# Attention: q and k kept by halves of the sequence, the first pair's groups as q, k, k, q, scores nine steps ahead of the values

## The chip, the cores and the metric

The kernel runs on one core of one Trainium2 chip. A core has five engines that each work through their own list of instructions in order: TensorE (PE, matmuls and transposes), VectorE (DVE), ScalarE (ACT), GpSimd (POOL) and SyncE (SP, which issues the DMAs here). They meet at semaphores. On-chip memory is SBUF (128 partitions) and PSUM (where PE writes, in banks of 512 fp32 columns).

The metric is the time of one execution on the device, in microseconds (us). The kernel before takes 2181.59 us, the median of 3 executions between 2181.50 and 2181.69.

## The reference

A decoder trunk of two layers on one sequence of 1024 tokens, width 1024, in fp32. Layer 0 mixes the tokens with a gated recurrent block, layer 1 with stick-breaking attention (16 heads of 64); a dense SwiGLU block of 2816 stands behind each. The change touches only the attention:

```python
def stick_breaking_attention(x, w_qkv, w_o):
    qkv = jnp.einsum("bsd,de->bse", x, w_qkv).reshape(bsz, seq, 3, N_HEADS, HEAD_DIM)
    q, k, v = ...
    for blk in range(seq // Q_BLOCK):        # Q_BLOCK = 128
        t0, t1 = blk * Q_BLOCK, (blk + 1) * Q_BLOCK
        z = jnp.einsum("bhqd,bhkd->bhqk", q[:, :, t0:t1], k[:, :, :t1]) * scale
        strict = jnp.arange(t1)[None, :] < t0 + jnp.arange(Q_BLOCK)[:, None]
        log_fail = jnp.where(strict, jax.nn.log_sigmoid(-z), 0.0)
        suffix = lax.cumsum(log_fail, axis=3, reverse=True) - log_fail
        weights = jnp.where(strict, jnp.exp(jax.nn.log_sigmoid(z) + suffix), 0.0)
        outs.append(jnp.einsum("bhqk,bhkd->bhqd", weights, v[:, :, :t1]))
    o = ...
    return jnp.einsum("bse,ed->bsd", o, w_o)
```

## The kernel before

**Precision.** An fp32 product is made of three matmuls: each operand is split into a part `hi` that PE's fp32r format holds and a remainder `lo`, and PE adds hi·hi, hi·lo and lo·hi (`mm3`, lines 141 to 143). Splitting takes a cast on ACT (`hi`) and a subtraction on DVE (`lo`).

**Two streams on PE.** The attention works through 8 pairs of heads. Two kinds of work are woven together by hand: the *fill*, which makes q, k and v of the next pair, and the *iterations*, which make scores, weights and values of the current pair. The whole stretch stands in a `manual_schedule` (line 1619): each engine executes its instructions in the order in which the Python code emits them, with no scheduler between.

**The fill** is the generator `qkv_steps` (line 1410). A pair has six groups: q, k and v (`which` 0, 1, 2), each for two halves of the sequence (`n`, 512 tokens). A group has 8 steps, a step is one `mm3` of 512 columns, so a pair has 48 steps. At the start of each `which`, `next_weights` queues the splitting of the weight block that comes next (three pieces in the list `later`, of which one is emitted per step), and `load_link` issues the load of the block after that, `raw` (three buffers). Behind a group `evacuate` (line 1440) takes the sum out of PSUM: DVE multiplies by `rbc[n]` (the row's 1/rms, spread over the partitions) into `t`; one step later ACT and DVE split `t` into `two`, and four DMAs on SP's queue spread it: q's into the tiles `Q` (lines 1466 and 1467; hi on 64 partitions and lo on the other 64, for each of the two heads), k's into `KK` (line 1470; hi and lo side by side, the same on both halves of the partitions). One score is then two matmuls that contract over all 128 partitions.

**An iteration** of the main loop (line 1645) emits, in this order: the score matmuls of one *chunk* (`z_part`, into one of two PSUM banks of the pool `psZ`); the PE transposes of a *unit* of weights two iterations ahead of its use (`t_part`) and their split (`t_split`: cast `th` on ACT, subtraction `tl` on DVE); the chunk's sigmoid on ACT and scan on DVE (`z_rest`, lines 1516 to 1522); one piece from `later`; two fill steps; in the last pair, steps of the output projection (`out_fill`) as `amount` says; an extra chunk in the iterations listed in `gains`; and the value matmuls of the unit (`av_part`). A head has 12 chunks (`chunk_list`, line 1494): eight on the diagonal, for query blocks j = 0 to 7 (those with j ≥ 4 read the second half of q and of k), then four off the diagonal, with the second half of q and the first of k. A head also has 12 units. `LEAD` says how many iterations the chunks run ahead of the units: 8, and by the three `gains` 11 within the last pair.

**The start.** Before the main loop the first pair's fill runs alone for 34 steps (line 1631), as nothing else is there to do: q half 0 and 1, k half 0 and 1, and two steps of v. The row statistics are not ready when q's groups end, so q's evacuations are put off (`waiting`) and the table `between` emits them at set steps: statistics at 12 and 16, the spreading of the result (`broadcast_r`) at 17 and 21, q's evacuations at 18 and 22. q's groups take the two `psZ` banks, which are idle then; k's and v's use the pool `psQ`.

## Time and profile before

| | |
|---|---|
| device time, median of 3 | 2181.59 us (2181.50 to 2181.69) |
| the profiled execution's own time | 2181.29 us |
| its span in the profile | 2179.5 us |
| granted clock of TensorE, mean | 0.999 |
| bytes moved by DMA | 277.64 MB, mean 127 GB/s |
| waits of `qk_ps` matmuls (the fill) on anything, largest group | 0.0 us |
| transfers `kk<-two` (64, 256 KB each) | 3.9 us from issue to landing |
| transfers `q<-two` (64, 128 KB each) | 2.3 us from issue to landing |

The span is the time from the first to the last instruction that the profiler saw. In the rows that follow, a busy time is the time in which an engine had an instruction in work. A row of the timeline has start and duration in us, engine, operation with its line, and the tiles written and read (`out<-in`); what stands in brackets behind it is the idle time of that engine just ahead, and what ended it. A row by stretches has the window, its length, and then for each engine (PE, its weight loads, DVE, ACT, POOL) the busy time and the count of instructions; behind these the granted clock, the share of the DMA engines that was busy, and GB/s. In a row on DMA issues, the first three times are the issue's own in ns, and the line under it the time to landing. The attention lies between 970 and 1450 us.

### The profile page before, as it was taken

The page shows a single profiled execution, that of the slowest core. Times are in us where ns is not written, and L with a number is a line of the kernel's source. Part 1 is how long each engine was busy: PE and PEld are TensorE (multiplying, and loading weights), DVE is VectorE, ACT ScalarE, POOL GpSimd, SP SyncE. Part 2 cuts the span into 40 slices and gives each one's busy share as a digit, 9 for nine tenths or more (in the row PEclk, how much of TensorE's full clock was granted, in tenths as well). Part 3 has the DMA queues.
Part 4 walks back from the last instruction along what each step waited for, and adds up shares of the span by engine and source line. Part 5 has one row for each costly group of instructions (what it writes and reads, how often), then busy time and mean ns, then how long its engine had stood idle before and what let it go on. Part 6 is the DMA issues. An engine that isn't in the chain of part 4 may idle for free.

```text
span 2179.5 us, 27426 instructions
## 1 busy us (share of the span) xinstructions
PE 2165.6 (99%) x10126; PEld 1802.2 (83%) x10126; DVE 1703.6 (78%) x2380; ACT 1077.0 (49%) x1765; POOL 112.2 (5%) x84
## 2 busy tenths in 40 slices
PE   8999999999999999999999999999999999999998
PEld 7888888888888888888888888888888888888887
DVE  7888777767777887887888888886877777788886
ACT  6677445334444544554555555553534444454556
POOL 1222020000000000000000000002000000000002
PEclk9999999999999999999999999999999999999999
DMA  7111412344444764434333344552133444467452
GB/s 233 49 49 39 135 39 73 103 125 157 138 146 139 248 222 130 146 121 101 98 97 93 95 105 107 147 193 57 53 116 122 146 145 145 141 232 233 138 153 89
DMA packets 296101, 277.64 MB, mean 127 GB/s; under 512 B 15256, under 2 KB 210976, under 8 KB 295968
## 3 DMA queue, kind: packets, MB, share of 16 engines
q1 hardware_dynamic: 295808, 275.64, 41.1%
q8 instruction: 79, 1.29, 0.3%
q14 instruction: 54, 0.44, 0.1%
q10 hardware_dynamic: 160, 0.27, 0.0%
HBM read 175.71 MB, written 74.97 MB: 115 GB/s over the span
## 4 chain that ended last, share of the span: by engine, by line
PE 96%; DVE 2%; ACT 1%; DMA 1%; issue 0%; SPq 0%; DVEq 0%; ACTq 0%
PE p_ps L143 18%; PE p_ps L141 18%; PE p_ps L142 18%; PE qk_ps L141 4%; PE qk_ps L143 4%; PE qk_ps L142 4%; PE wt_ps L1533 3%; PE a_ps L142 3%; PE a_ps L143 3%; PE a_ps L141 3%; PE ob_ps L141 3%; PE ob_ps L142 2%; PE ob_ps L143 2%; PE z_ps L1503 2%; PE z_ps L1504 2%; PE av_ps L1555 2%
## 5 line engine op out<-in xcount | busy, mean ns | idle before, releaser
L143 PE MATMUL p_ps<-vh,wbl 128*128 128x512 f32 x524 | 204.2, 390 | 0.2 <-DVE wbl L721 0.2
L143 PE MATMUL p_ps<-vh,wal 128*128 128x512 f32 x524 | 204.1, 389 | 0.1
L141 PE MATMUL p_ps<-vh,wbh 128*128 128x512 f32 x524 | 204.2, 390 | 0.0
L141 PE MATMUL p_ps<-vh,wch 128*128 128x512 f32 x524 | 204.1, 390 | 0.0
L143 PE MATMUL p_ps<-vh,wcl 128*128 128x512 f32 x524 | 204.1, 389 | 0.0
L142 PE MATMUL p_ps<-vl,wbh 128*128 128x512 f32 x524 | 203.9, 389 | 0.0
L142 PE MATMUL p_ps<-vl,wch 128*128 128x512 f32 x524 | 203.9, 389 | 0.0
L142 PE MATMUL p_ps<-vl,wah 128*128 128x512 f32 x524 | 203.9, 389 | 0.0
L141 PE MATMUL p_ps<-vh,wah 128*128 128x512 f32 x524 | 203.8, 389 | 0.0
L1542 ACT CAST th<-wt_ps 128x512 fp32r<-128x512 f32 x192 | 92.1, 480 | 209.6 <-PE wt_ps L1533 209.5
L717 ACT CAST wbh<-sb 128x1024 fp32r<-128x1024 f32 (+2 forms) x69 | 69.6, 1009 | 194.1 <-DVE sb L701 194.1
L1543 DVE TENSOR_TENSOR tl<-wt_ps,th 128x512 fp32r<-128x512 f32 x192 | 106.1, 552 | 62.9 <-ACT th L1542 61.1
L141 PE MATMUL qk_ps<-vh,whi 128*128 128x512 f32 x264 | 118.3, 448 | 0.0
L143 PEld LDWEIGHTS p_ps<-vh,wbl 128*128 128x128 f32 x524 | 98.4, 188 | 21.9 <-DVE wbl L721 1.5
L143 PEld LDWEIGHTS p_ps<-vh,wal 128*128 128x128 f32 x524 | 98.4, 188 | 21.4 <-DVE wal L712 1.0
L143 PEld LDWEIGHTS p_ps<-vh,wcl 128*128 128x128 f32 x524 | 98.4, 188 | 21.0 <-DVE wcl L731 0.6
L141 PEld LDWEIGHTS p_ps<-vh,wch 128*128 128x128 f32 x524 | 98.4, 188 | 20.5 <-ACT tb L1108 0.2
L141 PEld LDWEIGHTS p_ps<-vh,wbh 128*128 128x128 f32 x524 | 98.4, 188 | 20.4 <-ACT ta L1108 0.2
L142 PEld LDWEIGHTS p_ps<-vl,wah 128*128 128x128 f32 x524 | 98.4, 188 | 20.4
L141 PEld LDWEIGHTS p_ps<-vh,wah 128*128 128x128 f32 x524 | 98.4, 188 | 20.4
L142 PEld LDWEIGHTS p_ps<-vl,wbh 128*128 128x128 f32 x524 | 98.4, 188 | 20.3
L142 PEld LDWEIGHTS p_ps<-vl,wch 128*128 128x128 f32 x524 | 98.4, 188 | 20.3
(353 smaller groups left out, 5568.2 us busy)
## 6 DMA issues: line engine op xcount, KB each, us to landing
raw<-in_ffn_w_in SPq DMA_DIRECT2D x88, 512.0 KB, 4.0
vl<-pd SPq DMA_DIRECT2D x128, 256.0 KB, 3.5
pd<-U SPq DMA_DIRECT2D x90, 256.0 KB, 2.3
kk<-two SPq DMA_DIRECT2D x64, 256.0 KB, 3.9
raw<-in_ffn_w_out SPq DMA_DIRECT2D x56, 256.0 KB, 3.4
raw<-in_attn_w_qkv SPq DMA_DIRECT2D x24, 512.0 KB, 4.3
q<-two SPq DMA_DIRECT2D x64, 128.0 KB, 2.3
raw<-in_lru_w_in SPq DMA_DIRECT2D x15, 512.0 KB, 4.1
```

Of the source, the lines that this page charges most:

```text
L141: nc.tensor.matmul(ps, lhsT=wh, rhs=mh, start=first, stop=False, **kw)
L142: nc.tensor.matmul(ps, lhsT=wh, rhs=ml, start=False, stop=False, **kw)
L143: nc.tensor.matmul(ps, lhsT=wl, rhs=mh, start=False, stop=last, **kw)
L717: nc.scalar.copy(self.full(self.wb), self.full(self.sb))
L1503: nc.tensor.matmul(ps[:, 0 : c1 - c0], lhsT=lhsT, rhs=KK[q][hx][:, 0, c0:c1], start=True, stop=False)
L1504: nc.tensor.matmul(ps[:, 0 : c1 - c0], lhsT=lhsT, rhs=KK[q][hx][:, 1, c0:c1], start=False, stop=True)
L1533: nc.tensor.transpose(tp[:, c : c + P], W[q, hx, j, kb // 4][:, (kb % 4) * P : (kb % 4 + 1) * P], ident)
L1542: nc.scalar.copy(th[:, q0:], tp[:, q0:])
L1543: nc.vector.tensor_sub(tl[:, q0:], tp[:, q0:], f32(th)[:, q0:])
L1555: nc.tensor.matmul(ps[:, q0:], lhsT=VV[q][:, kb, hx], rhs=tl[:, q0:], start=False, stop=last)
```

## The change

The tiles of q and k are cut in two, one per half of the sequence: `Q[q]` of 1024 columns with four buffers becomes `Q[q, n]` of 512 with eight, `KK[q]` of 2 x 1024 likewise `KK[q, n]` of 2 x 512. A k transfer therefore writes one run of 1024 fp32 on each of 64 partitions, and no longer two runs of 512. The bytes, the number of DMAs, matmuls and other instructions stay.

In the first pair the groups run in the order q half 0, k half 0, k half 1, q half 1, v. The two first ones, q half 0 and k half 0, are put off and wait in `psZ`; q half 1 is evacuated in the ordinary way. The loads and splits of coming weight blocks move along with the groups. The first fill loop has 32 steps, `LEAD` is 9, and there are two extra chunks, so that the lead within the last pair is 11 as before.

```diff
         def qkv_steps(q):
-            for which in range(3):
-                w, at = wq.pop((q, which)), 3 * q + which + 1
-                if at < 3 * NP:
-                    wq[divmod(at, 3)] = next_weights(raws.pop(at))
+            groups = [(which, n) for which in range(3) for n in range(NH)]
+            if q == 0:
+                groups[1:4] = groups[2], groups[3], groups[1]
+            w = {}
+            for which, n in groups:
+                if which not in w:
+                    w[which] = wq.pop((q, which))
+                if n == 0 if q or which == 2 else (which, n) in ((0, 0), (0, 1)):
+                    at = 3 * q + which + 1 + (n if q == 0 else 0)
+                    if at < 3 * NP:
+                        wq[divmod(at, 3)] = next_weights(raws.pop(at))
+                    else:
+                        mix[0].w[mix[0].order[0]] = next_weights(mix[0].raw.pop(0))
+                    for i in (at + 1,) if at < 3 * NP else (at + 1, at + 2):
+                        load_link(i)
+                early = q == n == 0 and which < 2
+                ks = (1, 5, 2, 6, 3, 7, 0, 4) if (q, which) == (0, 0) else range(ND)
+                pool, tag = (psZ, "z") if early else (psQ, "qk")
+                ps = pool.tile([P, NB], F32, tag=tag, name="qk_ps")
+                wh, wl = w[which]
+                for i, k in enumerate(ks):
+                    mm3(ps, wh[:, k], wl[:, k], xh[k][n], xl[k][n], i == 0, i == ND - 1)
+                    if i == 5 and late:
+                        late.pop()()
+                    if i < ND - 1:
+                        yield
+                ev = evacuate(q, which, n, ps)
+                if early:
+                    waiting.append(ev)
+                    yield
                 else:
-                    mix[0].w[mix[0].order[0]] = next_weights(mix[0].raw.pop(0))
-                for i in (at + 1,) if at < 3 * NP else (at + 1, at + 2):
-                    load_link(i)
-                ks = (1, 5, 2, 6, 3, 7, 0, 4) if (q, which) == (0, 0) else range(ND)
-                for n in range(NH):
-                    pool, tag = (psZ, "z") if (q, which) == (0, 0) else (psQ, "qk")
-                    ps = pool.tile([P, NB], F32, tag=tag, name="qk_ps")
-                    for i, k in enumerate(ks):
-                        mm3(ps, w[0][:, k], w[1][:, k], xh[k][n], xl[k][n], i == 0, i == ND - 1)
-                        if i == 5 and late:
-                            late.pop()()
-                        if i < ND - 1:
-                            yield
-                    ev = evacuate(q, which, n, ps)
-                    if (q, which) == (0, 0):
-                        waiting.append(ev)
-                        yield
-                    else:
-                        next(ev)
-                        yield
-                        next(ev, None)
+                    next(ev)
+                    yield
+                    next(ev, None)
         def evacuate(q, which, n, ps):
-            full = lambda tag, m: [ap.tile([P, m, S], F32R, tag=tag, name=tag, bufs=4) for _ in range(2)]
+            halves = lambda tag, m: [ap.tile([P, m, NB], F32R, tag=tag, name=tag, bufs=8) for _ in range(2)]
             t = ap.tile([P, NB], F32, tag="t", name="t", bufs=2)
             cs = slice(n * NB, (n + 1) * NB)
             if which == 2:
@@ -1453,21 +1463,21 @@
             else:
                 nc.vector.tensor_mul(t, ps, rbc[n])
                 yield
-            if which == 0 and n == 0:
-                Q[q] = [t[:, 0] for t in full("q", 1)]
-            if which == 1 and n == 0:
-                KK[q] = full("kk", 2)
+            if which == 0:
+                Q[q, n] = [t[:, 0] for t in halves("q", 1)]
+            if which == 1:
+                KK[q, n] = halves("kk", 2)
             if which < 2:
                 two = ap.tile([P, 2, NB], F32R, tag="two", name="two", bufs=2)
                 nc.scalar.copy(two[:, 0], t)
                 nc.vector.tensor_sub(two[:, 1], t, f32(two)[:, 0])
                 for hx, (a, b) in enumerate(((top, bot), (bot, top))):
                     if which == 0:
-                        nc.sync.dma_start(f32(Q[q][hx])[a, cs], f32(two)[a, 0])
-                        nc.sync.dma_start(f32(Q[q][hx])[b, cs], f32(two)[a, 1])
+                        nc.sync.dma_start(f32(Q[q, n][hx])[a], f32(two)[a, 0])
+                        nc.sync.dma_start(f32(Q[q, n][hx])[b], f32(two)[a, 1])
                     else:
                         for half_ in (top, bot):
-                            nc.sync.dma_start(f32(KK[q][hx])[half_, :, cs], f32(two)[a])
+                            nc.sync.dma_start(f32(KK[q, n][hx])[half_], f32(two)[a])
                 return
             if n == 0:
                 VV[q] = ap.tile([P, NT, 2, P], F32R, tag="v", name="v", bufs=2)
@@ -1499,9 +1509,11 @@
         def z_part(q, hx, j, ci, c0, c1, diag):
             nk = (j + 1) * P
             ps = psZ.tile([P, NB], F32, tag="z", name="z_ps")
-            lhsT = Q[q][hx][:, j * P : (j + 1) * P]
-            nc.tensor.matmul(ps[:, 0 : c1 - c0], lhsT=lhsT, rhs=KK[q][hx][:, 0, c0:c1], start=True, stop=False)
-            nc.tensor.matmul(ps[:, 0 : c1 - c0], lhsT=lhsT, rhs=KK[q][hx][:, 1, c0:c1], start=False, stop=True)
+            lhsT = Q[q, j // 4][hx][:, j % 4 * P : (j % 4 + 1) * P]
+            for i in range(2):
+                nc.tensor.matmul(
+                    ps[:, 0 : c1 - c0], lhsT=lhsT, rhs=KK[q, ci][hx][:, i, 0 : c1 - c0], start=i == 0, stop=i == 1
+                )
             return ps
@@ -1587,7 +1599,7 @@
         heads = [(q, hx) for q in range(NP) for hx in range(2)]
         chunks = [c for q, hx in heads for c in chunk_list(q, hx)]
         units = [u for q, hx in heads for u in unit_list(q, hx)]
-        LEAD = 8
+        LEAD = 9
         def all_fill():
             yield from first
@@ -1626,17 +1638,17 @@
                 16: lambda: stats(rbc[1], psO, "o", 1),
                 17: lambda: broadcast_r(psO, "o", 0),
                 18: lambda: [*waiting[0]],
+                19: lambda: [*waiting[1]],
                 21: lambda: broadcast_r(psO, "o", 1),
-                22: lambda: [*waiting[1]],
             }
-            for i in range(1, 2 * ND * NH + 3):
+            for i in range(1, 2 * ND * NH + 1):
                 next(first)
                 if i in between:
                     between[i]()
-                if i > 4 and later:
+                if i > 3 and later:
                     later.pop(0)()
-            gains = [len(units) - x for x in (31, 29, 27)]
+            gains = [len(units) - x for x in (31, 28)]
             last_two, out_work = len(units) - 2 * 12, out_fill()
             amount = {x: 2 for x in (-1, 0, 1, 9, 10, 11, 12)}
```

What it does to the order, at three places. **SP, first pair.** SP issues the DMAs one after the other; `q` and `kk` are transfers of q and k into their tiles, `raw` the loads of weight blocks, `hd` belongs to the residual stream. Before:

```order
L114 DMA raw_7661<-in_attn_w_qkv 128x8x128
L1092 DMA hd0_1_121<-h0_1_1900 128x512
L1092 DMA hd4_0_128<-h4_0_1907 128x512
L1466 DMA q_7679<-two_7681 64x512
L1467 DMA q_7679<-two_7681 64x512
L1466 DMA q_7680<-two_7681 64x512
L1467 DMA q_7680<-two_7681 64x512
L1466 DMA q_7679<-two_7711 64x512
L1467 DMA q_7679<-two_7711 64x512
L1466 DMA q_7680<-two_7711 64x512
L1467 DMA q_7680<-two_7711 64x512
L1470 DMA kk_7726<-two_7728 64x2x512 x2
```

With the change:

```order
L1092 DMA hd0_1_121<-h0_1_1900 128x512
L1092 DMA hd4_0_128<-h4_0_1907 128x512
L1476 DMA q_7674<-two_7676 64x512
L1477 DMA q_7674<-two_7676 64x512
L1476 DMA q_7675<-two_7676 64x512
L1477 DMA q_7675<-two_7676 64x512
L1480 DMA kk_7688<-two_7690 64x1024 x2
L1480 DMA kk_7689<-two_7690 64x1024 x2
L1480 DMA kk_7720<-two_7722 64x1024 x2
L1480 DMA kk_7721<-two_7722 64x1024 x2
L114 DMA raw_7731<-in_attn_w_qkv 128x8x128
L1476 DMA q_7770<-two_7772 64x512
```

All of k's transfers moved ahead of q's second half, and the load of the next pair's q weights (raw_7661 before, raw_7731 now) moved from ahead of q's transfers to behind k's.

**ACT, the first scores.** `w0`, `w1` and so on are the sigmoids of the first pair's chunks, `whi` the casts of the weight block that SP's list shows as `raw`, `two` the casts of an evacuation. Before:

```order
L1462 CAST two_7762<-t_7760 128x512
L1397 CAST whi_7769<-raw_7661 128x512 x2
L1516 ACT_TABLE_LOAD
L1516 ACTIVATE w0_7786<-z_ps_7783 128x128
L1516 ACTIVATE w1_7799<-z_ps_7796 128x256
L1516 ACTIVATE w2_7811<-z_ps_7808 128x384
L1516 ACTIVATE w3_7827<-z_ps_7824 128x512
```

With the change:

```order
L1528 ACTIVATE w0_7767<-z_ps_7764 128x128
L1472 CAST two_7772<-t_7762 128x512
L1528 ACTIVATE w1_7793<-z_ps_7790 128x256
L1397 CAST whi_7779<-raw_7731 128x512
L1528 ACTIVATE w2_7806<-z_ps_7803 128x384
L1397 CAST whi_7779<-raw_7731 128x512
L1528 ACTIVATE w3_7820<-z_ps_7817 128x512
```

The cast of q's second half and the two casts of the next weight block stood ahead of the first sigmoid and stand between the sigmoids now.

**DVE, k's second half in the second pair.** `t` and `two` are the evacuation's multiplication and subtraction; between them stand the subtraction of a unit (`tl`) and a chunk's scan (`w`). Before:

```order
L1454 TENSOR_TENSOR t_8307<-qk_ps_8232,rbc1_82 128x512
L1543 TENSOR_TENSOR tl_8319<-wt_ps_8314,th_8318 128x384
L1522 SCALAR_TENSOR_TENSOR w_8322<-w_8322,w7_8220 128x512
L1463 TENSOR_TENSOR two_8325<-t_8307,two_8325 128x512
L1543 TENSOR_TENSOR tl_8352<-wt_ps_8348,th_8351 128x256
L1519 SCALAR_TENSOR_TENSOR w0_8355<-w0_8355,unit_7566 128x128
```

With the change:

```order
L1464 TENSOR_TENSOR t_8319<-qk_ps_8244,rbc1_82 128x512
L1555 TENSOR_TENSOR tl_8331<-wt_ps_8326,th_8330 128x384
L1531 SCALAR_TENSOR_TENSOR w0_8334<-w0_8334,unit_7566 128x128
L1473 TENSOR_TENSOR two_8339<-t_8319,two_8339 128x512
L1555 TENSOR_TENSOR tl_8366<-wt_ps_8362,th_8365 128x256
L1531 SCALAR_TENSOR_TENSOR w1_8369<-w1_8369,unit_7566 128x256
```

The chunks moved one iteration forward against the fill, so the scan ahead of the subtraction is that of the next head's first chunk, 128 columns, in place of one of 512.

## The prediction

> **What bounds the kernel now.** I read the busy times first, then the same by stretches, then TensorE (PE) instruction by instruction wherever a stretch is short of full, then the chain of waits behind those places.

> ```profile
> span 2179.5 us, 27426 instructions
> PE 2165.6 (99%) x10126; PEld 1802.2 (83%) x10126; DVE 1703.6 (78%) x2380; ACT 1077.0 (49%) x1765; POOL 112.2 (5%) x84
> ...
> 980.00:990.00 10.00, 8.99 (x43) 7.25 (x42) 4.28 (x7) 4.29 (x8) 0.00 (x0) 1.00 0.93 217
> ...
> 1100.00:1200.00 100.00, 100.00 (x543) 85.00 (x543) 85.84 (x126) 51.41 (x112) 4.57 (x6) 1.00 0.36 95
> ...
> 1425.00:1450.00 25.00, 23.77 (x136) 19.67 (x135) 22.68 (x33) 15.05 (x33) 2.57 (x2) 1.00 0.38 131
> ```

> PE sets the time, and the change leaves it the same matmuls in other places. In the middle of the attention (the row from 1100) it is never idle, so nothing can be won there. Two stretches of the attention are short: one at the first scores, one in the last pair. That caps the gain, so each is read row by row.

> ```profile
> 984.24 0.39 PE L142 MATMUL qk_ps<-xg,whi 128*128 128x512 f32 x1
> 984.47 0.39 PE L143 MATMUL qk_ps<-xg,wlo 128*128 128x512 f32 x1
> 985.86 0.36 PE L1503 MATMUL z_ps<-kk,q 128*128 128x256 f32 x1 [1.01 <-DMA kk<-two]
> ...
> 992.72 0.28 PE L1503 MATMUL z_ps<-kk,q 128*128 128x256 f32 x1
> ```

> Matmuls start every 0.23 us, so the first score could have started at 984.70. It started at 985.86: **1.16 us** lost to the DMA that spreads k.

> ```profile
> 1428.04 0.28 PE L1504 MATMUL z_ps<-kk,q 128*128 128x256 f32 x1
> 1428.63 0.33 PE L1533 MATMUL wt_ps<-ident,w 128*128 128x128 f32 x1 [0.30 <-DVE tl L1543]
> ...
> 1429.26 0.28 PE L1504 MATMUL z_ps<-kk,q 128*128 128x256 f32 x1
> 1429.81 0.66 PE L1533 MATMUL wt_ps<-ident,w 128*128 128x128 f32 x4 [0.26 <-DVE tl L1543]
> ...
> 1430.72 0.34 PE L1504 MATMUL z_ps<-kk,q 128*128 128x384 f32 x1
> 1431.71 0.65 PE L1533 MATMUL wt_ps<-ident,w 128*128 128x128 f32 x4 [0.66 <-DVE tl L1543]
> ```

> From score to transpose 0.59, 0.55 and 0.99 us pass, where some 0.12 to 0.17 would do: **1.7 us** behind VectorE (DVE). Both losses together are 2.9 us, 0.13% of the time.

> **The first scores.** The chain behind the first loss:

> ```profile
> 973.09 0.70 DVE t L1454
> 973.86 0.63 ACT two L1462
> 974.51 0.69 DVE two L1463
> 975.21 1.20 DVE wlo L1398 x2
> ...
> 981.16 0.65 SPq L1470
> 981.86 3.87 DMA kk<-two
> 985.86 0.36 PE z_ps L1503
> ```

> One evacuation is multiply, cast, subtract: 973.09 to 975.20. Before, weights and both halves of q stand ahead of k. Now k's first half is next: multiply at 975.1, cast 975.9, subtract 976.5 to 977.2, first kk DMA at about 977.26. The score needs two DMAs, the second landing 0.70+3.87 us after the first issue: 981.8. PE asks after 32 fill steps in place of 34, two steps of 3 x 0.23 us sooner: 983.3. The data is there 1.5 us early. **Gain 1.16 us**; k half 1's own two land well ahead of its chunk.

> **What is late next.** Moving k forward also moves what stands behind it. The weight block of the next pair (raw_7731) went out before q's DMAs; now it follows all eight of kk. The price of that queue:

> ```profile
> L1470 SPq DMA_DIRECT2D kk<-two x1: 1198/1198/1198, 987.7 to 987.7; - x1
> DMA to landing us min/median/max: 4.8/4.8/4.8
> ...
> L114 SPq DMA_DIRECT2D raw<-in_attn_w_qkv x1: 1321/1321/1321, 990.1 to 990.1; - x1
> DMA to landing us min/median/max: 6.3/6.3/6.3
> ...
> 987.00:992.00 5.00, 5.00 (x25) 4.20 (x24) 3.16 (x5) 1.85 (x5) 0.00 (x0) 1.00 0.98 230
> 992.00:995.50 3.50, 3.50 (x18) 2.92 (x18) 2.46 (x4) 0.82 (x3) 0.00 (x0) 1.00 1.01 280
> ```

> The DMA engines (the share before the last number) are full there. Eight kk transfers took from the first issue, 981.16, to the eighth landing, 987.7+4.8 = 992.5: 11.35 us. The two weight blocks behind them were in at 990.1+6.3 = 996.4, so 1.95 us each. Now the second kk group is ready at 980.1 (copy of rbc1, multiply, cast, subtract: 977.2 + 4 x 0.7), before the first group is through, so the queue does not run dry: eighth kk in at 977.26+11.35 = 988.6, weight block at **990.55**.

> Who waits? ScalarE (ACT) casts half of that block between the second and third sigmoid, and runs in order. Cast and sigmoid:

> ```profile
> 984.83 1.13 ACT L1397 CAST whi<-raw 128x512 fp32r<-128x512 f32 x2
> ...
> 989.73 0.49 ACT L1516 ACTIVATE w<-z_ps 128x384 f32<-128x384 f32 x1 [1.35 <-PE z_ps L1504]
> ```

> So 990.55 + 0.5 + 0.49 = 991.5, when the third chunk's psZ bank comes free; there are two banks, and the fifth chunk takes that one. PE wants it 6.8 us after the first chunk (985.86 to 992.72, less the restart): 983.3+6.8 = 990.1. **Loss 1.4 us.** The fifth chunk also needs q's second half, queued behind the same block: two DMAs of half a kk each, landing around 991.7, the same again and in parallel. The bounds: nothing, if the kk transfers, now one run of 4 KB a partition and not two of 2 KB, went as fast as the weight loads (0.5 MB in 1.95 us, so 0.98 us each and not some 1.18 us [(11.35 - 3.1)/7, a first one landing after 3.1 us]): then all is 1.5 us sooner. At the top 2.0 us, if the second group goes out late. I take 1.4, since both patterns write 64 partitions and the row of the old one is the nearest.

> ```profile
> DMA to landing us min/median/max: 3.1/3.1/3.1
> ```

> [...]

> **One more step of lead.** Score chunks move one iteration forward against the fill, so every k and q is needed one iteration sooner after it is made.

> ```profile
> L1470 SPq DMA_DIRECT2D kk<-two x1: 590/590/590, 1101.5 to 1101.5; - x1
> ...
> 1106.77 0.39 PE L1503 MATMUL z_ps<-kk,q 128*128 128x512 f32 x1
> 1109.23 0.33 PE L1503 MATMUL z_ps<-kk,q 128*128 128x256 f32 x1
> ...
> 1099.63 1.28 DVE L1522 TENSOR_TENSOR_SCAN w<-w,w 128x512 f32<-128x512 f32 x1
> 1100.82 0.67 DVE L1463 TENSOR_TENSOR two<-t,two 128x512 fp32r<-128x512 f32 x1
> ...
> 1101.74 0.42 DVE L1519 TENSOR_TENSOR_SCAN w<-w,unit 128x128 f32<-128x128 f32 x1
> ```

> In pair 2 (counted from 0) k's second half goes out at 1101.5, lands 4.57 us later (as above) at 1106.1, and its first chunk runs at 1109.23: 3.1 us to spare. One iteration costs 2.46 of them. The scan ahead of the subtract is now the short one (0.42 for 1.28 us), which gives 0.86 back. Left: 1.5 us, so pairs 1 to 6 wait for nothing. Without the 0.86 it is 0.7, still cover. The last pair, where chunks come faster:

> ```profile
> 1399.78 3.29 SPq L1470 DMA_DIRECT2D kk<-two  x4
> ...
> 1402.99 0.39 PE L1503 MATMUL z_ps<-kk,q 128*128 128x512 f32 x1
> ```

> Landing 1399.78+4.57 = 1404.35, less 0.86 = 1403.5; the chunk that needs it now stands where an iteration starts at 1402.99, plus 0.23 for the wider chunks ahead (512 columns, two matmuls of 0.23; 256 columns half). **Loss 0.3 us**, bounds 0 and 1.1 (no help from the scan).

> The lead's own benefit is nothing: DVE has slack in the middle (85.84 of 100) and PE no idle time there.

> **The last pair's 1.7 us stay.** The order is the old one again, on every engine, from iteration 166 on (about 1415 us), and DVE comes to rest after that:

> ```profile
> 1426.23 0.69 DVE L1543 TENSOR_TENSOR tl<-wt_ps,th 128x512 fp32r<-128x512 f32 x1 [0.70 <-ACT th L1542]
> ```

> Its 0.70 us of idle just ahead of the stalls wipe out whatever was done sooner. Two extra chunks for three change nothing behind it: 0, bounds -1.7 and +0.5.

> **Sum:** -1.16 + 1.4 + 0.3 + 0 = +0.5 us. The profiled execution took 2181.29 us (1.8 around the span), so 2181.8; the median shown, 2181.59, is 0.3 above it, so 2182.1.

> **Rivals.** (B) The queue clears in time, by the lower bound of the second part: -1.16 + 0.3, **2180.7 us**. For it: one kk DMA came in after 3.1 us and not 4.8, so part of the landing is queueing that a faster run would shorten, and the two weight loads did reach the rate that B needs; against it, those loads wrote 128 partitions, kk writes 64. [...] (C) Slower: k's second half misses its chunk in every pair. Place: the first chunk of 512 to 1023; it decides once the landing slips by more than 1.5 us, for instance because DVE runs its subtract an operation later. Another 1.28 us scan and one kk DMA (1.18) would be 2.5, so 1.0 us of wait in six pairs and 1.1 + 1.0 in the last: 2181.59 + 0.24 + 6.0 + 2.1 = **2189.9 us**. Against it: nothing new stands ahead of that subtract in the order. (D) The last pair's stalls go, since DVE enters it lighter: 2180.7 - 1.7 = **2179.0 us**; against it stands the idle row.

> **How the numbers follow.** Forecast 0.50, B 0.30, C 0.10, D 0.10. The forecast's own range is 2181.0 to 2183.4 (queue 0.7 to 2.0, last pair 0 to 1.1). Both signs hold much of the chance, so the range takes in B and D whole and, at the upper end, the forecast with both bounds and a C that strikes in two pairs only (2183.4 + 2 x 1.0 = 2185.4): 2179.0 to 2185.0; what is left out is most of C. About 0.2% (4.4 us) is what a measurement of this kernel can tell from no change: the forecast, B and D lie within it, C does not. Below 2177.2 no case leads, since the two losses are 2.9 us in all; 0.03 stays there for what I don't see. Slower 0.10, same 0.87.

> **What will show it.** Right: the first score follows the fill with no gap; the third sigmoid runs late, after a cast that waited for the raw DMA, and the fifth chunk's matmul waits 1 to 2 us for ACT or for q; the same three waits stand in the last pair, on DVE. The kk transfers take about 1.2 us each in a burst. Wrong: no wait at the fifth chunk (B), waits on kk in pairs 1 to 6 (C), or no DVE waits near 1430 us (D).

## The result

The changed kernel takes 2185.24 us (median of 21 executions, 2182.18 to 2187.49), the kernel before on the same chip 2181.50 us (21 executions, 2180.17 to 2182.80). The ratio is 1.0018, with a 95% interval from 1.0011 to 1.0024: slower by 3.7 us. The forecast was 2182.1 with a range of 2179.0 to 2185.0, so the time lies just above the range. The sign of the forecast was right and its size was not.

The executions of the changed kernel spread over 5.3 us, those of the kernel before over 2.6 us. The first thing to see in the page of the changed kernel is that TensorE is busy for longer with the same instructions:

```profile
span 2183.3 us, 27435 instructions
PE 2167.3 (99%) x10126; PEld 1803.0 (83%) x10126; DVE 1702.0 (78%) x2380; ACT 1079.7 (49%) x1765; POOL 112.3 (5%) x84
```

There are 10126 instructions, as before, and they keep TensorE busy for 1.7 us more (2165.6 before). The view by stretches says where:

```profile
980.00:990.00 10.00, 8.73 (x41) 6.99 (x39) 2.42 (x4) 1.62 (x4) 0.00 (x0) 1.00 1.04 243
990.00:1000.00 10.00, 7.97 (x27) 6.58 (x28) 6.31 (x9) 3.10 (x7) 0.00 (x0) 0.66 0.47 107
1000.00:1400.00 400.00, 400.00 (x2147) 339.05 (x2145) 337.55 (x495) 207.40 (x441) 13.73 (x18) 1.00 0.36 94
1400.00:1425.00 25.00, 24.83 (x134) 20.80 (x133) 22.56 (x33) 12.85 (x28) 1.09 (x1) 1.00 0.85 264
1425.00:1450.00 25.00, 23.78 (x135) 19.72 (x134) 23.69 (x32) 15.27 (x34) 3.66 (x3) 1.00 0.49 167
```

From 1000 to 1400 us TensorE never waits, and the last two stretches are short by 0.17 and 1.22 us. The rest of the attention's idle time, 1.27 and 2.03 us, lies between 980 and 1000 us, and from 990 us on the granted clock, the column before the last two, shows 0.66. TensorE's timeline there:

```profile
981.56 0.39 PE L143 MATMUL qk_ps<-vh,wlo 128*128 128x512 f32 x1
981.79 0.40 PE L1514 MATMUL z_ps<-kk,q 128*128 128x256 f32 x2
...
988.34 0.39 PE L143 MATMUL qk_ps<-vh,wlo 128*128 128x512 f32 x1
992.03 0.77 PE L1514 MATMUL z_ps<-kk,q 128*128 128x256 f32 x2 [3.30 <-ACT w L1528]
992.59 0.63 PE L141 MATMUL qk_ps<-vh,whi 128*128 128x512 f32 x1
993.02 0.63 PE L142 MATMUL qk_ps<-vl,whi 128*128 128x512 f32 x1
```

The first score follows the fill 0.23 us later, with no gap. The fifth chunk should start at 988.34 + 0.23 = 988.57 and starts at 992.03: 3.46 us of waiting. Behind it a matmul of 512 columns takes 0.43 us from start to start and not 0.23. ScalarE's timeline names what the wait was for:

```profile
983.84 0.38 ACT L1528 ACTIVATE w<-z_ps 128x256 f32<-128x256 f32 x1 [0.46 <-PE z_ps L1514]
990.88 0.62 ACT L1397 CAST whi<-raw 128x512 fp32r<-128x512 f32 x1 [6.66 <-DMA raw<-in_attn_w_qkv]
991.41 0.48 ACT L1528 ACTIVATE w<-z_ps 128x384 f32<-128x384 f32 x1
```

The cast stands idle for the weight block, and the third sigmoid is queued behind the cast. Cut into stretches of 3.41 us, TensorE's busy time (first number after the length) and its clock (third from the end) read:

```profile
987.57:990.98 3.41, 1.16 (x6) 0.62 (x4) 0.00 (x0) 0.10 (x1) 0.00 (x0) 1.00 1.13 242
990.98:994.39 3.41, 2.36 (x7) 2.01 (x8) 2.47 (x3) 2.13 (x5) 0.00 (x0) 0.50 1.00 241
994.39:997.81 3.42, 3.42 (x11) 2.74 (x10) 2.91 (x6) 0.39 (x1) 0.00 (x0) 0.50 0.02 6
997.81:1001.22 3.41, 3.41 (x21) 2.92 (x20) 1.19 (x2) 1.08 (x2) 0.00 (x0) 1.00 0.02 5
```

After a stretch that was busy for only 1.16 us, the clock was halved for two stretches, 6.83 us. Two pieces of the chain of waits complete the account, the first evacuation's multiplication and the load of the weight block:

```profile
971.54 0.70 DVE t L1464
...
983.12 7.74 DMA raw<-in_attn_w_qkv
```

The first evacuation began at 971.54, and at 973.09 in the profile of before: 1.55 us of the comparison come from the start of the program, which differs between executions of one kernel (in the five profiles of the change, below, this evacuation began between 971.54 and 973.70). The sum of the two profiles: -1.55 for the start, -1.16 for the first score, +3.46 for the fifth chunk, +0.33 in the last pair, and +2.73 for the slow clock (from the fifth chunk's start to the eighth's 8.06 us, against 5.33 in the run with one load moved, below). That makes +3.8, and the spans differ by 3.8 (2183.3 - 2179.5).

### The profile page after: what moved, and what is told of

It reads as the page before. It is cut to its first block, busy times and chain, and to the rows that moved or that the text cites. A ratio compares the mean times of both kernels' runs of the same rounds, so it can differ in the third digit from the quotient of the medians.

```text
span 2183.3 us, 27435 instructions
## 1 busy us (share of the span) xinstructions
PE 2167.3 (99%) x10126; PEld 1803.0 (83%) x10126; DVE 1702.0 (78%) x2380; ACT 1079.7 (49%) x1765; POOL 112.3 (5%) x84
## 4 chain that ended last, share of the span: by engine, by line
PE 95%; DVE 2%; ACT 1%; DMA 1%; issue 0%; SPq 0%; DVEq 0%; ACTq 0%
PE p_ps L143 18%; PE p_ps L141 18%; PE p_ps L142 18%; PE qk_ps L141 4%; PE qk_ps L143 4%; PE qk_ps L142 4%; PE z_ps L1514 3%; PE wt_ps L1545 3%; PE a_ps L142 3%; PE a_ps L143 3%; PE a_ps L141 3%; PE ob_ps L142 2%; PE ob_ps L141 2%; PE ob_ps L143 2%; PE av_ps L1567 2%; PE av_ps L1566 1%
## 5 line engine op out<-in xcount | busy, mean ns | idle before, releaser
L143 PE MATMUL p_ps<-vh,wbl 128*128 128x512 f32 x524 | 204.2, 390 | 0.2 <-DVE wbl L721 0.2
L143 PE MATMUL p_ps<-vh,wal 128*128 128x512 f32 x524 | 204.1, 389 | 0.1
L143 PE MATMUL p_ps<-vh,wcl 128*128 128x512 f32 x524 | 204.1, 389 | 0.0
L142 PE MATMUL p_ps<-vl,wch 128*128 128x512 f32 x524 | 203.9, 389 | 0.0
L142 PE MATMUL p_ps<-vl,wbh 128*128 128x512 f32 x524 | 203.9, 389 | 0.0
L142 PE MATMUL p_ps<-vl,wah 128*128 128x512 f32 x524 | 203.9, 389 | 0.0
L143 PEld LDWEIGHTS p_ps<-vh,wbl 128*128 128x128 f32 x524 | 98.4, 188 | 21.9 <-DVE wbl L721 1.4
L143 PEld LDWEIGHTS p_ps<-vh,wal 128*128 128x128 f32 x524 | 98.3, 188 | 21.3 <-DVE wal L712 1.0
L143 PEld LDWEIGHTS p_ps<-vh,wcl 128*128 128x128 f32 x524 | 98.4, 188 | 21.0 <-DVE wcl L731 0.6
L142 PEld LDWEIGHTS p_ps<-vl,wah 128*128 128x128 f32 x524 | 98.4, 188 | 20.4
L142 PEld LDWEIGHTS p_ps<-vl,wch 128*128 128x128 f32 x524 | 98.4, 188 | 20.4
L142 PEld LDWEIGHTS p_ps<-vl,wbh 128*128 128x128 f32 x524 | 98.4, 188 | 20.3
```

The lines of the kernel that those rows point to most:

```text
L142: nc.tensor.matmul(ps, lhsT=wh, rhs=ml, start=False, stop=False, **kw)
L143: nc.tensor.matmul(ps, lhsT=wl, rhs=mh, start=False, stop=last, **kw)
```

## The experiments

**One load moved (e1_load_early).** The weight block goes out at fill step 16, ahead of all of q's and k's transfers, as before the change; all else is the change.

```diff
                     for i in (at + 1,) if at < 3 * NP else (at + 1, at + 2):
-                        load_link(i)
+                        if i != 3:
+                            load_link(i)
+                if (q, which, n) == (0, 1, 1):
+                    load_link(3)
```

> The change with one load moved: the next pair's q weights are issued ahead of all of q's and k's transfers again, as before the change. Theory (one load in the wrong place): the cast on ScalarE no longer waits, and q's second half, with 0.5 MB less ahead of it, lands some 2 to 4 us sooner; the fifth chunk waits 0.5 us or less, the granted clock stays 1.0, and the time is the one before less 1.16 plus 0.3, so about 2180.7 us against 2181.5. Rival (the queue of k's eight transfers alone makes q's second half late): the fifth chunk still waits 2 us or more, now for q, and the time stays at 2183 or above.

Measured: 2180.52 us, against 2181.36 for the kernel before. TensorE's and ScalarE's timelines of this run:

```profile
989.92 0.62 PE L1517 MATMUL z_ps<-kk,q 128*128 128x512 f32 x2
991.73 0.40 PE L1517 MATMUL z_ps<-kk,q 128*128 128x256 f32 x2
```

```profile
987.29 0.61 ACT L1397 CAST whi<-raw 128x512 fp32r<-128x512 f32 x1
988.74 0.49 ACT L1531 ACTIVATE w<-z_ps 128x384 f32<-128x384 f32 x1 [0.84 <-PE z_ps L1517]
```

The fifth chunk no longer waits, the cast doesn't either, and the clock is 1.0. One load, in the wrong place in the queue, made up the whole of the loss. Against the kernel before, the gain of 0.84 us is too small to tell from nothing (ratio 0.9996, 0.9987 to 1.0005).

**TensorE kept busy (e2_keep_busy).**

```diff
+                if c == 5:
+                    warm = psT.tile([P, NB], F32, tag="T", name="warm_ps")
+                    k0 = KK[0, 0][0]
+                    for i in range(15):
+                        nc.tensor.matmul(warm, lhsT=k0[:, 0, 0:P], rhs=k0[:, 0], start=True, stop=True)
                 for a in some:
                     z = z_part(*a)
```

> The change with 15 matmuls of 512 columns more (3.45 us at 0.23 us each) ahead of the fifth chunk, whose sums nobody reads: TensorE is busy where it waited. Theory (the idle time cuts the granted clock in half for 6.83 us, which costs 3.2 us beside the wait itself): the fifth chunk's matmul starts as late as before, but the clock stays 1.0 and the matmuls behind it take 0.23 us again, so the time falls by about 3 us from that of a cut run, to about 2182. Rival (the slow matmuls behind the wait come from something else, such as the transfers that run then): they still take 0.43 us, and the time stays at 2185.

Measured: 2184.36 us (2182.73 to 2186.03). TensorE's timeline, its stretches, and ScalarE's timeline:

```profile
989.16 3.56 PE L1664 MATMUL warm_ps<-kk 128*128 128x512 f32 x15
992.56 0.40 PE L1514 MATMUL z_ps<-kk,q 128*128 128x256 f32 x2
```

```profile
988.00:992.00 4.00, 4.00 (x19) 3.30 (x18) 1.35 (x2) 2.02 (x4) 0.00 (x0) 1.00 1.14 249
992.00:994.00 2.00, 2.00 (x12) 1.67 (x11) 2.00 (x4) 0.28 (x1) 0.00 (x0) 1.00 1.19 290
```

```profile
989.61 0.62 ACT L1397 CAST whi<-raw 128x512 fp32r<-128x512 f32 x1 [4.79 <-DMA raw<-in_attn_w_qkv]
```

The chunk started as late, 3.4 us behind the fill, but the clock stayed 1.0 with the DMA engines just as busy (1.14 and 1.19): in this run the transfers alone did not cut it. The number in the expectation was wrong. The 15 matmuls cost their 3.4 us whether or not the data was late, and the sum is 2181.36 - 1.16 + 3.4 + 0.3 = 2183.9. In this execution, one of the fastest of eleven (2182.95), the load was in at 989.61, 1.9 us sooner than in the profile of the change when counted from the first k transfer. The third sigmoid ended at 990.6, so without the added matmuls the chunk would have waited some 1.5 us (an estimate: 990.6 less 989.16). That the idle time cut the clock is therefore shown by the runs with copies on ScalarE, below (cut at 3.0 and 5.6 us of it, not at 1.7), and not by this one.

**The casts put off (e3_casts_later).** `if later and u >= 5 - LEAD:` ahead of the main loop's `later.pop(0)()`.

> The change with the split of the next weight block put off by five iterations, so that no cast stands between the first sigmoids; the DMAs stay. Theory (two things are late at about the same time, the cast that holds up the third sigmoid and q's second half): the fifth chunk waits for q's transfers now, nearly as long, 3 us or more; the time stays within 1 us of the change's 2185.2. Rival (the cast alone is at fault, q's half would be in time): the wait falls below 1 us, the clock stays 1.0, and the time is 2181.5 or less.

Measured: 2185.29 us. TensorE's timeline:

```profile
995.39 0.47 PE L1514 MATMUL z_ps<-kk,q 128*128 128x256 f32 x2 [3.06 <-DMA q<-two]
```

With the cast out of the way, the chunk waits 3.2 us for q's second half, and the clock is halved for 3.41 us. The block made two things late at once, and moving the cast alone cures nothing.

**The old lead (e4_old_lead).** `LEAD = 8`, 34 fill steps, `gains` at 31, 29, 27, with the change's halves and order.

> The change with the old lead: 34 fill steps ahead of the first score, eight iterations of lead, three extra chunks; the halves and the order q, k, k, q stay. Theory: PE asks for the fifth chunk 1.38 us later, so it waits 1.38 us less (some 2.0 us); that is too short to cut the clock; the 0.3 us wait for k in the last pair is gone. Time: 2181.5 - 1.16 + 2.0 = about 2182.3. Rival (any wait at this place cuts the clock): 0.43 us matmuls for 6.83 us, and about 2185. Other rival (the lead is at fault for all of it): 2180.3.

Measured: 2188.57 us (5 executions). None of the three theories had this. TensorE's and ScalarE's timelines:

```profile
995.99 1.01 PE L1514 MATMUL z_ps<-kk,q 128*128 128x384 f32 x2 [6.30 <-ACT w L1528]
```

```profile
993.21 1.14 ACT L1397 CAST whi<-raw 128x512 fp32r<-128x512 f32 x2 [6.70 <-DMA raw<-in_attn_w_qkv]
994.37 1.28 ACT L1528 ACT_TABLE_LOAD   x1
995.66 0.55 ACT L1528 ACTIVATE w<-z_ps 128x128 f32<-128x128 f32 x2
```

Two more fill steps emit two pieces of `later` before the first sigmoid. So the casts, which wait for the load, hold up the first sigmoid, and the third chunk finds no bank: 6.3 us of idle time, and a halved clock for 10.24 us. The expectation had moved the request and left the cast where it was.

**Load early, old lead (e5_early_old_lead, and again e12_early_old_lead_again).** The edits of the first and the fourth run together.

> Halves and q, k, k, q, with the weight block issued early (as in the run with one load moved) and the old lead of eight with 34 fill steps and three extra chunks. Theory: the first score follows the fill with no gap (1.16 us won), no cast waits for a load, so neither the third nor the fifth chunk waits, and the k wait in the last pair (0.37 us, seen in all four kernels with a lead of nine and not in the one with eight) is gone: before less 1.16, about 2180.2 us, 0.4 less than with the lead of nine. Rival (the six waits of the run with the old lead came from the lead itself and not from the cast ahead of the first sigmoid): a wait of several us at the third chunk stays, and the time is 2185 or more.

> The version with the weight block issued early and the old lead once more, for a second profile and a second comparison. Theory: no wait at the first, third and fifth chunk and none for k in the last pair again; 1.2 to 1.3 us under the kernel before on the same chip (2179.91 against 2181.22 in the first comparison). Rival (that difference was the scatter of the start, which moves an execution by 1.6 us): as often above as below the kernel before, a difference under 0.5 us.

Measured: 2179.91 against 2181.22 (ratio 0.9996, 0.9987 to 1.0005), then 2180.01 against 2181.07 (0.9995, 0.9986 to 1.0003). By stretches, first profile:

```profile
980.00:990.00 10.00, 10.00 (x48) 8.37 (x47) 5.89 (x11) 4.46 (x8) 0.00 (x0) 1.00 1.01 237
990.00:1000.00 10.00, 10.00 (x55) 8.38 (x54) 7.47 (x11) 3.81 (x8) 0.00 (x0) 1.00 0.39 94
1400.00:1425.00 25.00, 25.00 (x142) 21.46 (x140) 22.84 (x32) 13.05 (x29) 1.96 (x2) 1.00 0.97 306
```

TensorE is full in all three. The medians are 1.31 and 1.06 us below those of the kernel before, where the 1.16 us of the first score were to be won. Each interval taken alone still holds 1. Only over both comparisons together, on two chips, is there a difference: the mean of 22 executions lies 0.99 us below that of 48 of the kernel before, with twice its standard error at 0.48. That is what speaks for this version as the better one.

**The lead alone (e6_lead_only).** The kernel before with `LEAD = 9`, 32 fill steps, `gains` at 31 and 28.

> The kernel before with nothing but the lead changed (32 fill steps, lead of nine, two extra chunks). Theory: the first score comes when k's transfers land, as before, but with two fill steps fewer done by then: 1.38 us lost, a wait of 2.5 us in place of 1.16; 0.37 us more in the last pair; together before plus 1.7, about 2183.1 us; 2.5 us of idle time leave the clock at 1.0. Rival (2.5 us are enough to cut the clock): 0.43 us matmuls behind the first score, and 2184.7 or 2186.3.

Measured: 2184.69 us (2182.58 to 2186.34): the rival was right. TensorE's timeline and stretches:

```profile
983.81 0.39 PE L143 MATMUL qk_ps<-vh,wlo 128*128 128x512 f32 x1
986.54 0.55 PE L1503 MATMUL z_ps<-kk,q 128*128 128x256 f32 x1 [2.35 <-DMA kk<-two]
```

```profile
983.14:986.55 3.41, 1.06 (x6) 0.60 (x4) 0.69 (x1) 0.00 (x0) 0.00 (x0) 1.00 0.97 222
986.55:989.96 3.41, 3.41 (x10) 2.83 (x11) 1.12 (x2) 0.83 (x2) 0.00 (x0) 0.50 0.36 86
```

The wait is 2.5 us, as expected, and it was enough: a stretch busy for 1.06 us, then one at half the clock. It did not do so every time: two of the eleven executions (2182.58 and 2182.79) had a mean granted clock of 1.000, and one stretch of 3.41 us at half the clock would take 0.0008 off it.

**The change again (e7_change_again, e13_change_look_a, e14_change_look_b, e15_change_look_c).** The changed kernel as it is, four more profiles.

> The changed kernel once more, for a second profile. Theory: the weight block's time from issue to landing differs between executions (7.8 us in the profile of the change, 5.9 and 6.7 us in two kernels with the same queue ahead of it); where it is near 5.9 the wait at the fifth chunk is near 1.5 us and the clock is not cut, and the execution takes some 2182.3 us; where it is near 7.8 the wait is near 3.5 us, the clock is cut for 3.41 or 6.83 us, and the execution takes 2185.5 to 2187.5. Rival (the wait is the same in all executions): 3.3 us or more and a cut clock whatever the landing.

> The changed kernel, a third profile. Theory: the wait at the fifth chunk follows the later of the weight block's landing plus a cast and a sigmoid, and q's second half; where the block lands about 13.3 us after the first k transfer's issue the wait is near 1.5 us and the clock stays 1.0, where it lands 15 us after it the wait is near 3.5 us and the clock is cut. Rival (wait and cut do not go together): a long wait without a cut, or a short one with it.

> The changed kernel, a fourth profile; the same expectations as for the third.

> The changed kernel, a fifth profile; the same expectations as for the third.

Measured, from the timelines of TensorE and ScalarE (the wait is the time from the start of the last matmul ahead to that of the fifth chunk, less 0.23; the load is the time from the issue of `raw` to the start of its cast):

| profile | load, us | wait at the fifth chunk, us | clock halved, us | device time, us |
|---|---|---|---|---|
| of the result | 7.76 | 3.46 | 6.83 | 2185.13 |
| e13 | 7.38 | 3.38 | 6.83 | 2186.99 |
| e7 | 7.42 | 3.48 | 3.41 | 2185.62 |
| e14 | 6.80 | 2.26 | 3.41 | 2184.72 |
| e15 | 6.46 | 2.29 | 3.41 | 2183.30 |

The shortest, e15, in ScalarE's and TensorE's timelines:

```profile
989.93 0.62 ACT L1397 CAST whi<-raw 128x512 fp32r<-128x512 f32 x1 [5.35 <-DMA raw<-in_attn_w_qkv]
```

```profile
991.22 0.48 PE L1514 MATMUL z_ps<-kk,q 128*128 128x256 f32 x2 [2.13 <-ACT w L1528]
```

The three loads of 7.4 us and more go with waits of 3.4 to 3.5 us, the two of 6.8 and less with 2.3 us, and at 2.3 us the clock was already cut. All five were cut. The expected execution, with a wait near 1.5 us and no cut, was not among them. Among the 21 executions of the result there are three whose mean granted clock is 1.000 (2182.18, 2182.91 and 2183.77), so they had no stretch at half the clock; how long they waited is not on record. In e7 the clock was halved once more, for 3.41 us at the start of the program, so its time holds more than the wait and its cut.

**The halves alone (e8_halves_only).** The kernel before with nothing but the tiles cut.

> The kernel before with nothing but the tiles of q and k cut in halves, so that a k transfer writes one run of 4 KB on each partition and not two of 2 KB. Theory (64 partitions and not the run's length set the rate): eight transfers still take some 1.18 us each behind the first, the first score waits 1.1 us as before, and the time is the one before within 0.3 us. Rival (longer runs are faster, as the weight loads' rate of 0.98 us per 256 KB would have it): the eighth k transfer lands 1.4 us or more sooner, the first score 0.2 to 0.4 us.

Measured: 2181.18 against 2181.22 us (ratio 1.0002, 0.9993 to 1.0011). The eighth k transfer in the view by tile, and the first score in the timeline:

```profile
L1470 SPq DMA_DIRECT2D kk<-two x1: 1172/1172/1172, 988.0 to 988.0; - x1
...
DMA to landing us min/median/max: 4.8/4.8/4.8
```

```profile
986.28 0.47 PE L1504 MATMUL z_ps<-kk,q 128*128 128x256 f32 x2 [0.85 <-DMA kk<-two]
```

The eighth still takes 4.8 us from issue to landing, 11.1 us after the first one's issue at 981.73 (11.35 before), and the first score still waits, 0.85 us of idle time for 1.01. Runs of 4 KB brought some 0.2 us at most.

**Idle time alone (e9_idle_short, e10_idle_long, e11_idle_shorter).** In the kernel with one load moved, 10, 14 and 8 copies of 512 columns on ScalarE ahead of the third sigmoid, into a tile that nobody reads:

```diff
+                if c == 3:
+                    slow = ap.tile([P, NB], F32, tag="slow", name="slow", bufs=1)
+                    for _ in range(10):
+                        nc.scalar.copy(slow, f32(xh[0][0]))
```

> The version with the weight block issued early, and ten copies of 512 columns (0.52 us each) on ScalarE ahead of the third sigmoid: the fifth chunk waits about 1.8 us for ScalarE, with no transfer late. Theory (the clock is judged over stretches of 3.41 us and cut when TensorE was busy for less than about a third of one): at 1.8 us of idle time at least 47% of any such stretch is busy, so the clock stays 1.0 and the time is 0.8 under the one before plus 1.8, about 2182.2 us. Rival (the cut needs only an idle time of some length, below 1.8 us): 0.43 us matmuls behind the wait, and 2183.8 us or more.

> The same with fourteen copies: the fifth chunk waits about 3.9 us for ScalarE. Theory: at least one stretch of 3.41 us is nearly idle, so the clock is cut in every execution, for 3.41 us or a multiple of it, at 1.6 us each: before less 0.8 plus 3.9 plus 1.6 or 3.2, about 2186.0 or 2187.6 us, with the matmuls behind the wait at 0.43 us. Rival (the transfers and their late landing, not the idle time, cut the clock): the clock stays 1.0 and the time is 2184.4 us.

> As the two runs with copies on ScalarE, with eight copies. They took 0.65 us each and not 0.52, so the waits were 3.0 and 5.6 us; eight leave 1.7 us. Theory (a stretch of 3.41 us that is busy for less than about a third cuts the clock): no stretch falls below half, the clock stays 1.0 in every execution, and the time is 2181.3 less 0.8 plus 1.7, about 2182.2 us. Rival (a wait of 1.7 us is enough): 0.43 us matmuls behind the wait, and about 2183.8 us.

Measured: 2184.91, 2187.45 and 2182.76 us. A copy took 0.65 us and not the 0.52 of the first two expectations, so the waits were 3.0, 5.6 and 1.7 us, and the run with ten copies did not test the wait of 1.8 us that it was made for; the one with eight did. By stretches, the run with ten copies, then the one with eight:

```profile
989.00:992.00 3.00, 0.17 (x2) 0.02 (x1) 0.04 (x1) 2.90 (x6) 0.00 (x0) 0.98 1.17 293
992.00:995.30 3.30, 3.30 (x9) 2.72 (x10) 3.30 (x5) 1.11 (x3) 0.00 (x0) 0.50 0.11 26
```

```profile
989.50:992.91 3.41, 1.89 (x10) 1.30 (x9) 0.61 (x1) 3.31 (x7) 0.00 (x0) 1.00 1.12 259
992.50:996.00 3.50, 3.50 (x19) 2.99 (x20) 3.50 (x5) 1.32 (x4) 0.00 (x0) 1.00 0.48 117
```

No wait in these runs is for a transfer, and the half clock lasts on while the DMA engines rest (0.11). At 3.0 and 5.6 us of idle time the clock was halved (for 3.41 and 6.83 us), at 1.7 us it was not, and no execution of that run took more than 2183.2 us.

## Why the prediction failed, point by point

- **What bounds the kernel: right.** TensorE, with two short stretches in the attention; the middle stayed full (400.00 of 400).
- **The first scores, a gain of 1.16 us: right.** The score came at 981.79; with the start's 1.55 us added that is 983.34, and 983.3 was forecast.
- **What is late next: right in place and cause.** The fifth chunk, held by the cast that waits for the weight block and, in parallel, by q's second half (the run with the casts put off). It asked at 988.57 + 1.55 = 990.1, as forecast.
- **The size of that wait: wrong, 1.4 us forecast, 2.3 to 3.5 measured.** The step that failed is the price of a weight block, "so 1.95 us each", taken from two loads in a row. It put the landing 13.3 us after the first k transfer's issue. In the run with TensorE kept busy it did land after 13.3 us, but in the five profiles of the change after 13.8 to 15.1. The k transfers ahead of it were not late: in the profile of the change the seventh landed 10.1 us after the first one's issue, and 10.3 us before. So it is the block that came late: counted from 11.35 us, where the prediction put the eighth k transfer, it took 2.5 to 3.8 us and not 1.95. In the row that gave the price nothing was queued behind the two loads; here q's transfers and two more blocks were. Whether that is the reason stays open. The bounds, 0 and 2.0 us, let the k transfers vary and left the load fixed. (The forecast's own range takes 0.7 and not 0 as the lower bound here, and by its terms both its ends would be 0.1 us higher; neither bears on the miss.)
- **The clock: missing, the second step that failed.** The sum charged the wait at its own length and let the matmuls behind it run at full speed, a term put at nothing without a reason. In the trace of before the only waits in the attention were 1.16 us and less, and none was followed by a slower clock (the full one is on record from 12.6 to 2176.7 us), so no row there showed the cut. From the fifth chunk's start to the eighth's, with the 5.33 us of the run with one load moved taken off, the cut cost 1.5 to 1.7 us where it lasted one stretch and 2.7 us where it lasted two, between four and eight tenths of the wait that set it off. In four of the five profiles (not in e7) this is the larger part of the miss: with its own wait of 1.4 the forecast was +0.5 us, with 2.3 to 3.5 it is +1.4 to +2.6, and the cut brings that to +2.9 to +5.3, around the +3.7 measured.
- **k's transfers keep their rate: right.** The halves alone changed nothing that could be measured in the time, and 0.2 us in the transfers where the lower bound needed 1.5, so the taken value, and not that bound, was the true one. That the 64 partitions, which both patterns write, set this rate is not shown: 256 KB of k took 1.18 us and 256 KB of a weight load, onto 128 partitions, 0.98 us, the halves alone changed the length of a run on the partition, and nothing changed their number.
- **The lead in pairs 1 to 6, no wait: right; in the last pair 0.3 us: right,** 0.33 in the profile of the change, none in the versions with a lead of eight. That it waits for k is argued: the profile names nothing for this wait. The chunk starts at 1407.17, 3.9 us after the issue of the second k transfer of that group (1403.3), and in the first pair the second k transfer took 3.9 us from issue to landing.
- **The last pair's 1.7 us stay: right.** The same three waits for VectorE, in TensorE's timeline of the change (0.30, 0.26 and 0.66 before):

```profile
1432.47 0.33 PE L1545 MATMUL wt_ps<-ident,w 128*128 128x128 f32 x1 [0.30 <-DVE tl L1555]
1433.65 0.66 PE L1545 MATMUL wt_ps<-ident,w 128*128 128x128 f32 x4 [0.27 <-DVE tl L1555]
1435.56 0.66 PE L1545 MATMUL wt_ps<-ident,w 128*128 128x128 f32 x4 [0.65 <-DVE tl L1555]
```

- **The rivals.** B, the queue that clears, did not come true in the change; moving one load reached its time (2180.52 for 2180.7), by another way than faster k transfers. C and D did not occur. None of them held a wait that slows what comes after it.

## What to carry to other kernels

When work moves forward in a queue, follow what it is moved past to its own consumer, and see whether that one stands, on an engine that runs in order, ahead of something that TensorE needs. A wait of TensorE had a second price here: in the profiles those of 2.3 us and more, which left it idle for 60% or more of a stretch of 3.41 us, were followed by half the clock, at a cost of 1.5 to 2.7 us beside the wait in the change, and those of 1.16 and 1.7 us were not. So two waits of 1.2 us may cost less than one of 2.4 (an estimate from these numbers; no run here has tried that). Take the spread of a DMA's landing from several bursts, with what is queued behind it, and not from the one case at hand.

## What the runs showed of the hardware

How long the cut lasted went with where the wait fell on the grid: the waits of the result's profile and of e7 were the same, 3.46 and 3.48 us. In the first the wait was spread over two stretches, busy for 1.16 and 2.36 us, and the clock was halved for 6.83 us. In the second, nearly all of it lay in one, busy for 0.46 us, the next was busy for 3.04 us, and the clock was halved for 3.41 us. A wait of 2.3 us was enough for a cut.

**The tail of the load came late.** The block consists of 1024 packets of 512 B, q's transfers behind it of packets of 2 KB. Packets that ended in each microsecond after the load's issue, from the trace's records (later 512 B packets belong to the next loads):

```
us after the issue        2-3  3-4  4-5  5-6   6-7
e2, 512 B packets         113  460  448    3    69
change, 512 B packets      93  473  409   36   103
change, 2 KB packets        0    0   42  101    93
```

In e2 all 1024 were through within 6 us. In the change 1011 were, and the last 13 came in among q's packets; the load landed 1.9 us later. Why they were late is open.
